# Moving operands in SBUF: new homes modulo 256 bytes for the context's tiles, the long operands and the first FFN's products

## The chip, the cores and the metric

The kernel runs on one core of a Trainium2 chip. A core has a matrix engine (TensorE, PE in the profile, with its weight loads listed apart as PEld), a vector engine (VectorE, DVE), a scalar engine (ScalarE, ACT), GpSimd (POOL), and queues for transfers between the chip's memory (HBM) and the on-chip buffer (SBUF). SBUF has 128 partitions; a tile is a range of bytes that is the same in each of them, and in this document its *home* is the byte address at which that range begins, often taken modulo 256. Sums of products go to PSUM. The metric is the device time of one execution in microseconds; of several executions the median counts.

## The reference

Two streams of tokens with 1024 features, 512 latent and 256 context tokens, go through two layers. Layer 0 mixes tokens by grouped-query attention (16 query heads, 4 key heads), layer 1 by a bidirectional Mamba-2 scan; a gated convolutional FFN of width 2816 follows each. All of it is float32.

```python
for i in range(2):
    h_l = rms_norm(x, w_mix[i]) * (1 + scale_l) + shift_l
    h_c = rms_norm(ctx, w_mix[i]) * (1 + scale_c) + shift_c
    o_l, o_c = attention(h_l, h_c) if i == 0 else mamba2(h_l, h_c)
    x += gate_l * o_l
    if i == 0: ctx += gate_c * o_c
    x += gate_l2 * ffn(modulated rms_norm of x)
    if i == 0: ctx += gate_c2 * ffn(modulated rms_norm of ctx)

def ffn(h):
    g, u = split(h @ w_up)              # 1024 -> 2 x 2816
    g = conv3(g) + b                    # along the tokens, per feature
    return (silu(g) * u) @ w_down       # 2816 -> 1024
```

The shifts, scales and gates come from two condition vectors (one for latent, one for context tokens) by a linear map per layer, six chunks of 1024 for each. The output is the latent stream `x`. The context is needed in the first layer and in the projections into the Mamba mixer, and no further.

## The kernel before

**Layout and products.** Activations lie feature-major: 8 tiles of 128 features by 512 latent or 256 context tokens. A float32 product is made of three products of rounded parts: weight and activation are each split into a rounded part and its remainder (`split`, L81 to L88: a cast on ACT, a subtraction on DVE), and `mm3` (L103 to L111) issues, for each block of 128 features, weight-high by activation-high (L108), weight-high by activation-low (L109), weight-low by activation-high (L111). The weight tile of 128 x 128 is loaded into TensorE for each of these; the activations (512 or 256 columns) move past it. In the profile `hh..` and `hl..` are the high and low parts of modulated activations, with the stage as the last letters: `a` attention, `f` FFN, `s` Mamba, `ol` and `oc` attention's output for latent and context tokens, `y` the first eight tiles of Mamba's output. `hdh`, `hdl` are the parts of the FFN's gated products, `yh`, `yl` those of the last eight tiles of Mamba's output.

**Rings.** Tiles come from pools. A tile that is asked for with a tag comes from a ring of a fixed number of buffers; a pool lays its rings and single tiles one behind the other in the order in which they are first asked for, each rounded up to 32 bytes, and a pool begins where the one before it ends. The pools in question, with the homes that the compiled program of the kernel before gives:

| pool and tile | bytes each x number | home modulo 256 |
|---|---|---|
| `const`: identity and selectors, parameters, ones, `sc32`, then 12 tiles `mod` and 4 `moda`, ... | `mod`: 64 x 12 | ends at 7264 |
| `p`, tag `h512`: long modulated tiles (latent tokens) | 2048 x 16 | 96 |
| `p`, tag `h256`: context's modulated tiles | 1024 x 16 | 96 |
| `p`, tag `t4`: weights as loaded, high, low | 4096 x 10 | 96 |
| `p`: `silu`, behind `t4` | 64 | 96 |
| `pa` (attention), `pf` (first FFN), `pg` (second FFN): all rings and tiles | multiples of 256 | 160 |
| `pt` (Mamba): `na`, one element, first in the pool | 32 | 160 |
| `pt`, tag `t3`: nine tiles of 3104 bytes | | eight residues 32 apart |
| `pt`, tag `t2`: 39 tiles of 2048 bytes, `yh` and `yl` among them | | 32 |

The pool `p` has a few small rings behind `silu`, and lasts for the whole kernel; `pa`, `pf`, `pt` and `pg` take turns in the space behind it.

**Order of work.** A scheduler orders each engine's instructions from the program as it is written (L406 to L515 of the attention are kept in the written order on PE, ACT and DVE). The stages, by time on the page's span: attention up to about 390 us; its output projection and the first FFN up to 972; the Mamba stage up to about 1500; the second FFN to the end.

- Attention (`attention`, L392): query and key projections `ps_l` for the latent and `ps_c` for the context tokens take their weights from slabs that lie in `pa`; four later query projections `ps_q` take them from `t4`. Attention's output projection is a `ps_d` with `hhol`, `hhoc`.
- FFN (`ffn`, L886): step `f` of 22 projects up twice (`ps_up`: 8 blocks x 3 terms of 512 columns, and in the first FFN the same of 256 columns for the context), convolves and gates on ACT and DVE into `hd` (L936 to L938), and splits `hd` into `hdh`, `hdl` (L939, L940). Latent and context tokens of the first FFN stand side by side in one tile of 768 columns, latent first. Two or three steps are a group, whose products are projected down (`down`, L856; `ps_d`) after the first up-projection of the next group. The last group is projected down in the order context, first latent half, second latent half (256 columns each), with the next norm interleaved; the first weights of the next stage read their halves as `ps_first`.
- Mamba (`ssd`, L969): `ps_in` is the projection in (six weight tiles for each of eight groups of heads, of which three, x twice and B, are for both streams), interleaved with the scan; `ps_wo` is the projection out, and sums eight tiles `y` in `h512` and eight in `pt`'s `t2` ring into one accumulation.

The condition chunks of layer 1 are computed by DVE during the first FFN (`ada_dve`, L156).

Of the kernel before, what the change touches and what calls it, by code (L numbers as in the profile page):

```python
# [7 lines left out]
P = 128  # L8
F32 = mybir.dt.float32
F32R = mybir.dt.float32r  # L10
# [6 lines left out]
KT = D // P  # L17
L = 512
C = 256
# [372 lines left out]
def attention(g, fill, X, late):  # L392
# [3 lines left out]
    S64 = slice(0, 64), slice(64, 128)  # L396
    Bk, Sb = (lambda name: Bank(g, name)), (lambda name: S(g, name))
    t2 = lambda name, dt=F32: g.t3p.tile([P, 512], dt, tag="t2", bufs=6, name=name)
    g.h = [[htiles(g, n, f"a{i}_{m}") for m in range(KT)] for i, n in enumerate((L, C))]
    hl, hc = g.h  # L400
    kn = g.par[:, PC["kn"] : PC["kn"] + 1]


# [52 lines left out]
    g.qn8 = g.const.tile([P, 1], F32, name="qn8")  # L456
    nc.vector.tensor_scalar(g.qn8, g.par[:, PC["qn"] : PC["qn"] + 1], HD ** -0.5, None, ALU.mult)

    e = g.p.tile([P, 2 * KT], F32, name="silu")
    nc.scalar.activation(e, g.cin, AF.Exp, scale=-1.0)  # L460
    nc.vector.tensor_scalar(e, e, 1.0, None, ALU.add)
    nc.vector.reciprocal(e, e)
# [423 lines left out]
def ffn(g, layer, streams, x, h, first, nxt=None, side=iter(()), after=()):  # L886

    nc, I = g.nc, g.I  # L890
    ns = len(streams)
    tot = sum(n for n, _ in streams)
    off = [0, L]

    cw = [g.par[:, PC[f"fw{layer}{t}"] : PC[f"fw{layer}{t}"] + NFT] for t in range(3)]
    cb = g.par[:, PC[f"fb{layer}"] : PC[f"fb{layer}"] + NFT]
    whole = [[(i, 0, n) for i, (n, _) in enumerate(streams)]]

    def gemm(t):

        if t % NFT == 0:
            ps = first[t // NFT]
        else:
            w = load_w(g, I["wup"][layer, t])
            if t % NFT == 1:
                out = []
                for i in range(ns):
                    ps = Bank(g, "ps_up1")
                    for _ in gemm_in(g, [(ps, w)], h, (0, 0), [[s] for s in whole[0] if s[0] == i]):
                        pass  # L910
                    out.append((ps, [i]))
                return [(ps[:, : streams[i][0]], off[i], off[i] + streams[i][0], i) for ps, (i,) in out]
            ps = S(g, "ps_up")
            for _ in gemm_in(g, [(ps, w)], h, off, [[s] for s in whole[0]]):
                pass
        return [(ps[:, :tot], 0, tot, None)]

    def up(f):
        pg = gemm(f)
        cv = t3(g, "cv", n=tot)  # L920
        w0, w1, w2 = (c[:, f : f + 1] for c in cw)
        for ps, a, b, _ in pg:
            nc.scalar.activation(cv[:, a:b], ps, AF.Identity, scale=w1, bias=cb[:, f : f + 1])
        for i in range(ns):
            a, b = off[i], off[i] + streams[i][0]
            ps, o = next((ps, o) for ps, o, e, j in pg if j in (None, i))
            nc.vector.scalar_tensor_tensor(cv[:, a + 1 : b], ps[:, a - o : b - o - 1], w0, cv[:, a + 1 : b], ALU.mult, ALU.add)
            nc.vector.scalar_tensor_tensor(cv[:, a : b - 1], ps[:, a - o + 1 : b - o], w2, cv[:, a : b - 1], ALU.mult, ALU.add)
        follow(g, nc.scalar.activation(cv, cv, AF.Silu))
        some = (2, 2, 2, 3)[f] if ns > 1 and f < 4 else 1  # L930
        for _ in range(some):
            next(side, None)
        pu = gemm(NFT + f)
        for _ in range(some):
            next(side, None)
        hd = t3(g, "hd", n=tot)  # L936
        for ps, a, b, _ in pu:
            nc.vector.tensor_tensor(hd[:, a:b], cv[:, a:b], ps, ALU.mult)  # L938
        hi, lo = t3(g, "hdh", F32R, n=tot), t3(g, "hdl", F32R, n=tot)  # L939
        split(g, hd, hi, lo)  # L940
        return [(hi[:, off[i] : off[i] + streams[i][0]], lo[:, off[i] : off[i] + streams[i][0]]) for i in range(ns)]

    gate = g.mod[layer][5]
    segs, f = [], 0
    for n in [3] + [2] * 8 + [3] if nxt else [2] * 11:
        segs.append(range(f, f + n))
        f += n
    acts, pend, wf = {}, None, []

    def flush(fs, order, norm=None, after=None):  # L950
        ws = [load_w(g, I["wdown"][layer, f * P : (f + 1) * P]) for f in fs]
        if after:
            wf.extend(firsts(g, *after))
        return down(g, ws, [acts.pop(f) for f in fs], gate, streams, x, order, norm, side=side)

    for fs in segs:
        for j, f in enumerate(fs):
            acts[f] = up(f)
            if j == 0 and pend:
                flush(pend, whole)  # L960
        pend = fs
    for _ in side:
        pass
    if nxt:
        ln_exp(g)
    return flush(pend, [[s] for s in ending(streams)], nxt, after), wf


def ssd(g, x, norm, wf, bg, close):  # L969
# [26 lines left out]

    H2 = 64
    ps = ps_dt
    na = small("na", [P, 1])
    follow(g, nc.scalar.activation(na, par("alog", 0), AF.Exp))  # L1000
    nc.vector.tensor_scalar(na, na, -1.0, None, ALU.mult)
    TH = T // 2
# [342 lines left out]
def body(nc, tc, I, out, dbg=None):  # L1345
# [25 lines left out]
    nc.vector.memset(g.sc32, 0.0)  # L1371
    tc.keep_in_program_order(nc.scalar.preload_act_table_set("natural_log_exp_and_others"))
    g.cin = g.par[:, PC["cc"] : PC["cc"] + 2 * KT]
    g.mod = [[g.const.tile([P, KT, 2], F32, name=f"mod{i}{c}") for c in range(6)] for i in range(2)]
    g.moda = [{c: g.const.tile([P, KT, 2], F32, name=f"moda{i}{c}") for c in (1, 4)} for i in range(2)]

    fill = Fill()
# [23 lines left out]
    first = first_tiles(g, wf, nrm, bg)  # L1401
    pha.close()
    phf = ExitStack()
    g.t3p, g.n3 = pool("pf", phf), 24


    def dump():
# [122 lines left out]
```

## Time and profile before

| | |
|---|---|
| median of 3 runs | 1873.63 us (1873.2 to 1874.46) |
| the profiled execution's own time | 1875.38 us |
| its span, first to last instruction | 1873.6 us |
| matmuls, busy time of TensorE | 11474, 1848.9 us (99%) |
| busy: weight loads, DVE, ACT, POOL | 1547.2, 1303.6, 807.3, 299.8 us |
| HBM read, written | 198.79 MB, 6.82 MB: 110 GB/s over the span |
| granted TensorE clock over the span | 0.998 |

The page names an instruction by line, engine, operation and `out<-in`, then its shape and count; behind the bar stand the group's busy time and the mean of one in ns, and then the idle time of the engine just before the group, with what ended it. A matmul's duration has the way through the array in it and overlaps the next one's; the distance from one start to the next is the pace.

### The profile page before, as it was taken

To read this page: it belongs to the slowest core of one execution; us is meant where nothing else is said; L and a number is where in the kernel's file an instruction comes from. 1 tells how busy PE (TensorE), PEld (TensorE's weight loads), DVE (VectorE), ACT (ScalarE), POOL (GpSimd) and SP (SyncE) were. 2 spreads that over 40 slices of the span, in tenths; PEclk is the share of its full clock that TensorE was granted. 3 is DMA by queue.
4 is the path that set the end of the run, shared out by engine and by line. 5 is a ranking of instruction groups with operands and counts; after the bars stand their busy time and mean duration, and the time that the engine had idled before them with its cause. 6 is when DMAs were issued, how large, how long until landed. Compare 5 with 4: busy or idle time off the path is not lost.

```text
span 1873.6 us, 28798 instructions
## 1 busy us (share of the span) xinstructions
PE 1848.9 (99%) x11474; PEld 1547.2 (83%) x11474; DVE 1303.6 (70%) x1950; ACT 807.3 (43%) x1402; POOL 299.8 (16%) x266
## 2 busy tenths in 40 slices
PE   9999999999999999999999999999999999999999
PEld 8876656798888888888888888888887888888887
DVE  6588888778787776544487787777797565565655
ACT  4534444363122222222367667776666352323231
POOL 2123120040000000000032333444443210000000
PEclk9999999999999999999999999999999999999999
DMA  9233151124444552211224432443352223222232
GB/s 345 76 109 101 63 178 52 57 84 164 146 135 145 191 185 99 68 58 56 68 91 141 124 105 87 124 124 113 124 178 93 79 91 97 95 95 97 90 103 89
DMA packets 74070, 211.67 MB, mean 113 GB/s; under 512 B 9040, under 2 KB 14544, under 8 KB 73808
## 3 DMA queue, kind: packets, MB, share of 16 engines
q1 hardware_dynamic: 73936, 209.84, 34.0%
q8 instruction: 90, 1.47, 0.3%
q14 instruction: 44, 0.36, 0.1%
HBM read 198.79 MB, written 6.82 MB: 110 GB/s over the span
## 4 chain that ended last, share of the span: by engine, by line
PE 84%; DVE 7%; issue 3%; DMA 2%; POOL 2%; ACT 2%; SPq 0%; DVEq 0%; POOLq 0%; ACTq 0%
PE ps_up L108 10%; PE ps_up L111 10%; PE ps_up L109 10%; PE ps_d L108 6%; PE ps_d L111 6%; PE ps_d L109 6%; PE ps_in L111 4%; PE ps_in L109 4%; PE ps_in L108 4%; PE ps_s L697 2%; PE ps_o L661 2%; PE ps_st L1123 2%; DMA wada<-in_adaA 1%; PE ps_wo L111 1%; PE ps_wo L108 1%
## 5 line engine op out<-in xcount | busy, mean ns | idle before, releaser
L87 DVE TENSOR_TENSOR wl<-wst,wh 128x1024 fp32r<-128x1024 f32 x207 | 258.5, 1249 | 233.9 <-PE ps_up L109 138.9
L85 ACT CAST wh<-wst 128x1024 fp32r<-128x1024 f32 x211 | 221.3, 1049 | 393.7 <-DMA wst<-in_wup 323.6
L108 PE MATMUL ps_up<-hhf,wh 128*128 128x512 f32 x1008 | 357.6, 355 | 0.0
L109 PE MATMUL ps_up<-hlf,wh 128*128 128x512 f32 x1008 | 357.3, 354 | 0.0
L111 PE MATMUL ps_up<-hhf,wl 128*128 128x512 f32 x1008 | 357.0, 354 | 0.0
L108 PEld LDWEIGHTS ps_up<-hhf,wh 128*128 128x128 f32 x1008 | 190.8, 189 | 26.4
L109 PEld LDWEIGHTS ps_up<-hlf,wh 128*128 128x128 f32 x1008 | 190.8, 189 | 26.3
L111 PEld LDWEIGHTS ps_up<-hhf,wl 128*128 128x128 f32 x1008 | 190.6, 189 | 26.4
L108 PE MATMUL ps_in<-hhs,wh 128*128 128x512 f32 (+1 forms) x560 | 204.4, 365 | 1.5 <-ACT dt L1008 1.5
L109 PE MATMUL ps_in<-hls,wh 128*128 128x512 f32 (+1 forms) x560 | 199.4, 356 | 0.0
L111 PE MATMUL ps_in<-hhs,wl 128*128 128x512 f32 (+1 forms) x560 | 198.7, 355 | 0.0
L108 PE MATMUL ps_d<-hdh,wh 128*128 128x512 f32 (+1 forms) x568 | 193.3, 342 | 0.2 <-ACT hdh L85 0.2
L111 PE MATMUL ps_d<-hdh,wl 128*128 128x512 f32 (+1 forms) x568 | 193.5, 341 | 0.0
L109 PE MATMUL ps_d<-hdl,wh 128*128 128x512 f32 (+1 forms) x568 | 192.9, 340 | 0.3 <-DVE hdl L87 0.3
L874 DVE SCALAR_TENSOR_TENSOR X<-ps_d,mod,X 128x512 f32<-128x512 f32 (+1 forms) x224 | 124.3, 583 | 35.9 <-PE ps_d L111 35.2
L108 PEld LDWEIGHTS ps_in<-hhs,wh 128*128 128x128 f32 x560 | 105.9, 189 | 16.6 <-ACT dt L1008 1.7
L109 PEld LDWEIGHTS ps_d<-hdl,wh 128*128 128x128 f32 x568 | 106.7, 188 | 14.8 <-DVE hdl L87 0.7
L111 PEld LDWEIGHTS ps_in<-hhs,wl 128*128 128x128 f32 x560 | 105.8, 189 | 14.7
L111 PEld LDWEIGHTS ps_d<-hdh,wl 128*128 128x128 f32 x568 | 106.6, 188 | 13.1
L108 PEld LDWEIGHTS ps_d<-hdh,wh 128*128 128x128 f32 x568 | 106.3, 188 | 13.4 <-ACT hdh L85 0.7
L109 PEld LDWEIGHTS ps_in<-hls,wh 128*128 128x128 f32 x560 | 106.0, 189 | 13.2
L700 ACT ACTIVATE pr<-ps_s 128x1024 f32<-128x1024 f32 x56 | 57.2, 1021 | 107.2 <-PE ps_s L699 107.2
(339 smaller groups left out, 3653.4 us busy)
## 6 DMA issues: line engine op xcount, KB each, us to landing
wst<-in_wup SPq DMA_DIRECT2D x88, 512.0 KB, 3.3
wada<-in_adaT SPq DMA_DIRECT2D x56, 512.0 KB, 3.3
wst<-in_win SPq DMA_DIRECT2D x48, 512.0 KB, 3.4
wst<-in_wdown SPq DMA_DIRECT2D x44, 512.0 KB, 3.5
E<-ad SPq DMA_DIRECT2D x64, 256.0 KB, 6.9
wada<-in_adaB SPq DMA_DIRECT2D x24, 512.0 KB, 4.1
ec<-ead SPq DMA_DIRECT2D x64, 128.0 KB, 5.6
wst<-in_wout SPq DMA_DIRECT2D x16, 512.0 KB, 3.3
```

The lines of the kernel that those rows point to most:

```text
L85: cast = keep(nc.scalar.copy(hi, src))
L87: keep(eng.tensor_tensor(lo, src, _r(hi), ALU.subtract))
L108: mm(out, wh, ah, start=first, stop=False)
L109: mm(out, wh, al, start=False, stop=False)
L111: mm(out, wl, ah, start=False, stop=last)
L661: nc.tensor.matmul(po[S64[e], :n], v, pr[:, 512 * e + off : 512 * e + off + n], start=first, stop=last)
L697: nc.tensor.matmul(outs[e], kk[e][a][S64[e], k], b[S64[e], q], start=i == 0, stop=False)
L700: exps.append(nc.scalar.activation(pr, ps, AF.Exp))
L874: nc.vector.scalar_tensor_tensor(ap, o[:, c0:c1], gate[:, m, v : v + 1], ap, ALU.mult, ALU.add)
L1123: nc.tensor.matmul(ps[:, d * 256 : (d + 1) * 256], Bt[:, t * P : (t + 1) * P], xw[d][t], start=t == ts[0], stop=t == ts[-1])
```

## The change

Nothing of the arithmetic changes. Five edits alter where tiles lie:

- the three modulation tiles `mod` 3, 4, 5 of layer 1 (64 bytes each) are asked for in pool `p`, between the long and the context tiles, instead of in `const`;
- `silu` (64 bytes) is asked for ahead of everything in `t4`, instead of behind it;
- `hdh` and `hdl` come from a ring of their own of 11 tiles; the `t3` ring of the first FFN goes from 24 tiles to 14 (the second FFN's stays at 24);
- in the first FFN a gap of 48 elements (192 bytes) stands between the latent and the context part of `hdh` and `hdl`, and the two parts are split by a cast and a subtraction each, instead of one of each for both;
- `na`, the Mamba pool's first tile, is asked for with 40 elements, of which one is used.

```diff
@@ attention
-    g.h = [[htiles(g, n, f"a{i}_{m}") for m in range(KT)] for i, n in enumerate((L, C))]
-    hl, hc = g.h
+    hl = [htiles(g, L, f"a0_{m}") for m in range(KT)]
+    for ch in (3, 4, 5):
+        g.mod[1][ch] = g.p.tile([P, KT, 2], F32, name=f"mod1{ch}")
+    hc = [htiles(g, C, f"a1_{m}") for m in range(KT)]
+    e = g.p.tile([P, 2 * KT], F32, name="silu")
+    g.h = [hl, hc]
...
-    e = g.p.tile([P, 2 * KT], F32, name="silu")
     nc.scalar.activation(e, g.cin, AF.Exp, scale=-1.0)
@@ ffn, up(f)
-        hi, lo = t3(g, "hdh", F32R, n=tot), t3(g, "hdl", F32R, n=tot)
-        split(g, hd, hi, lo)
-        return [(hi[:, off[i] : off[i] + streams[i][0]], lo[:, off[i] : off[i] + streams[i][0]]) for i in range(ns)]
+        gap = 48 * (ns - 1)
+        pair = [g.t3p.tile([P, (tot + gap + 63) // 64 * 64], F32R, tag="hd", bufs=11, name=nm) for nm in ("hdh", "hdl")]
+        hls = []
+        for i in range(ns):
+            a, b = off[i], off[i] + streams[i][0]
+            hls.append(tuple(t[:, a + i * gap : b + i * gap] for t in pair))
+        if ns == 1:
+            split(g, hd, *hls[0])
+            return hls
+        for i in range(ns):
+            split(g, hd[:, off[i] : off[i] + streams[i][0]], *hls[i])
+        return hls
@@ ssd
-    na = small("na", [P, 1])
+    na = small("na", [P, 40])[:, :1]
@@ body
-    g.mod = [[g.const.tile([P, KT, 2], F32, name=f"mod{i}{c}") for c in range(6)] for i in range(2)]
+    g.mod = [[g.const.tile([P, KT, 2], F32, name=f"mod{i}{c}") for c in range(3 if i else 6)] + [None] * (3 * i)
+             for i in range(2)]
...
-    g.t3p, g.n3 = pool("pf", phf), 24
+    g.t3p, g.n3 = pool("pf", phf), 14
```

## The prediction

> **What bounds the kernel now.** I read the page's busy times first, then the chain that ended last, then the busy time by stage, then the waits of TensorE. On the page, the busy shares and the chain's shares by engine; below them, by stage (window, its length, busy us and instruction count of PE, PEld, DVE, ACT, POOL, then clock and DMA), the first FFN and the Mamba stage; last, two of the longest waits of PE in the whole run (its total, how often, the longest once).
>
> ```profile
> PE 1848.9 (99%) x11474; PEld 1547.2 (83%) x11474; DVE 1303.6 (70%) x1950; ACT 807.3 (43%) x1402; POOL 299.8 (16%) x266
> PE 84%; DVE 7%; issue 3%; DMA 2%; POOL 2%; ACT 2%; SPq 0%; DVEq 0%; POOLq 0%; ACTq 0%
> 410.00:925.00 515.00, 514.69 (x2987) 454.80 (x2986) 339.16 (x516) 128.80 (x139) 1.48 (x2) 1.00 0.36 123
> 972.00:1400.00 428.00, 423.90 (x2499) 367.10 (x2498) 327.12 (x379) 296.61 (x627) 155.96 (x135) 1.00 0.40 121
> PE ps_xt L1097 <- DVE xf L1200: 1.8, 6, 0.5
> PE ps_ada L132 <- DMA wada<-in_adaA: 1.8, 1, 1.8
> ```
>
> TensorE is busy 99% of the span, its clock is granted in full (1.00 in both stages), and no wait in that list sums to more than 1.8 us. In the first FFN it lacks 0.3 us of 515, in the Mamba stage 4.1 us of 428. So the kernel ends when TensorE has issued its matmuls, and the only thing that moves the end is the pace of back-to-back matmuls: time per matmul times their number. This decides how I cost the change: nothing in it alters the number of matmuls, so I look for what sets their pace.
>
> **The pace depends on where the operands lie.** The compiled program of the kernel before gives every tile's address. All three-term products (L108, L109, L111) read their weights from the ring `t4`, which lies at 96 modulo 256 bytes. The moving operands lie at 96 too (tags h512 and h256: difference 0 from the weights), at 160 (tiles of the attention and FFN pools: difference 64) or at 32 (the Mamba pool's 2 KB ring: difference 192). Below, groups of the same shape (columns: instruction, its operands, its shape, count; busy us, mean ns of one). I take the L109 row of each trio; the L108 and L111 rows have the same counts.
>
> ```profile
> L109 PE MATMUL ps_up<-hlf,wh 128*128 128x512 f32 x672 | 262.2, 390 | 0.0
> L109 PE MATMUL ps_up<-hlf,wh 128*128 128x256 f32 x336 | 95.1, 283 | 0.0
> L109 PE MATMUL ps_in<-hls,wh 128*128 128x256 f32 x184 | 52.0, 283 | 0.0
> L109 PE MATMUL ps_first<-hlf,wh 128*128 128x256 f32 x80 | 22.8, 290 | 2.3 <-POOL hlf L301 1.5 <-DVE hlf L304 0.8
> L109 PE MATMUL ps_d<-hloc,wh 128*128 128x256 f32 x64 | 18.0, 283 | 0.0
> L109 PE MATMUL ps_q<-hla,wh 128*128 128x256 f32 x32 | 9.0, 281 | 0.0
> L109 PE MATMUL ps_c<-hla,wsh 128*128 128x256 f32 x48 | 13.3, 277 | 0.0
> L109 PE MATMUL ps_d<-hdl,wh 128*128 128x256 f32 x256 | 71.0, 279 | 0.3 <-DVE hdl L87 0.3
> L111 PE MATMUL ps_d<-hdh,wl 128*128 128x512 f32 x312 | 122.6, 393 | 0.0
> L109 PE MATMUL ps_l<-hla,wsh 128*128 128x512 f32 x48 | 19.8, 413 | 0.3 <-DVE hla L304 0.3
> L109 PE MATMUL ps_wo<-hly,wh 128*128 128x512 f32 x48 | 18.7, 390 | 0.0
> L109 PE MATMUL ps_wo<-yl,wh 128*128 128x512 f32 x48 | 18.9, 394 | 0.0
> L109 PE MATMUL ps_wo<-hly,wh 128*128 128x256 f32 x32 | 9.0, 282 | 0.0
> L109 PE MATMUL ps_wo<-yl,wh 128*128 128x256 f32 x32 | 8.9, 277 | 0.0
> ```
>
> Two pairs are controls. `ps_c` and `ps_q` read the same context tiles in the same stage; against the slabs (difference 192) one takes 277 ns, against `t4` (difference 0) 281. In `ps_wo` the tiles `hy` (difference 0) and `y` (192) are read by one accumulation with weights from one ring. There the order turns round with the width: of 256 columns the tile at 192 is quicker (277 against 282), of 512 columns the tile at 0 is (390 against 394). A row's mean has the pipeline's latency in it, so for the pace itself I take starts in the instructions by time. In `ps_wo` each run below is 24 matmuls long (8 blocks by 3 terms); the two `ps_up` rows bound one run of 24 in the first FFN.
>
> ```profile
> 903.45 0.28 PE L108 MATMUL ps_up<-hhf,wh 128*128 128x256 f32 x1
> ...
> 906.33 0.40 PE L108 MATMUL ps_up<-hhf,wh 128*128 128x512 f32 x1
> ...
> 1472.55 0.39 PE L108 MATMUL ps_wo<-yh,wh 128*128 128x512 f32 x1
> ...
> 1478.15 0.28 PE L108 MATMUL ps_wo<-hhy,wh 128*128 128x256 f32 x1
> ...
> 1481.02 0.29 PE L108 MATMUL ps_wo<-yh,wh 128*128 128x256 f32 x1
> ...
> 1483.76 0.28 PE L108 MATMUL ps_wo<-hhy,wh 128*128 128x256 f32 x1
> ...
> 1486.62 0.29 PE L108 MATMUL ps_wo<-yh,wh 128*128 128x256 f32 x1
> ```
>
> 256 columns at difference 0: 2.88 us / 24 = 120.0 ns in `ps_up`, 2.87 and 2.86 us / 24 = 119.4 in `ps_wo`. 256 columns at 192: 2.74 / 24 = 114.2 ns. 512 columns at 192: 5.60 / 24 = 233.3 ns. So a 256-column matmul gains 120.0 - 114.2 = 5.8 ns by going from 0 to 192, and a 512-column one about 4 ns a row by going the other way.
>
> A rule of the Trainium skill speaks against all this: in "TensorE: Matmul & The Clock Gate", section "Step-by-step: what each phase is for", TensorE has two independent SBUF read ports, and "Loading the next tile's weights doesn't steal SBUF read bandwidth from the running matmul". By that the homes would not matter and the sum below would be zero. The rows of `ps_wo` differ by 5 ns within one accumulation, so here I go by the rows; the rule is a rival further down.
>
> **The change part by part: where each operand lands.** A pool lays its tiles in order of first request. (1) Three modulation tiles of 64 bytes leave the constants and are asked for between the long and the context tiles, so the pool that holds h512, h256 and `t4` starts 192 bytes lower. h512 goes from 96 to 160. (2) h256 comes behind the three tiles and stays at 96. (3) The 64-byte `silu` tile now comes ahead of `t4`, which goes from 96 to 160. The sum of sizes is the same, so the pools behind do not move. Differences after: h512 to `t4` 160 - 160 = 0 as before, h256 to `t4` 96 - 160 = -64, which is 192 (before 0). Tiles of the attention and FFN pools stay at 160: difference 0 (before 64), and h512 against the slabs also 0 (before 192). (4) `na` grows from one to 40 elements (32 to 160 bytes), so the Mamba pool's ring goes from 32 to 160: `y` is at 0 (before 192). (5) The products `hdh`, `hdl` get a ring of their own; in the first FFN the context part is written 48 elements (192 bytes) later, so it lies at 192 (before 64).
>
> None of this adds an instruction or a DMA but (5), which splits each of the first FFN's products in two.
>
> **The sum**, counts times three for the three terms:
>
> - Context by h256, 0 to 192: `ps_up` 336 x 3 = 1008; `ps_in` 184 x 3 = 552; `hoc` 64 x 3 = 192; `ps_q` 32 x 3 = 96; of `ps_first` the context part, 2 weight tiles x 8 blocks in each of two stages, 2 x 16 x 3 = 96. Together 1944 x 5.8 ns = 11.3 us. The other 256-column `ps_first` (64 of the row's 80) are halves of the latent tokens, which stay at 0.
> - Long `hd`, 64 to 0: 312 x 3 = 936, 393 against 390 ns at most and equal rows at least: I take 2 ns, 1.9 us (0 to 2.8).
> - `hd` of 256 columns: 22 x 8 x 3 = 528 are context, 64 to 192. They stand at 279 with target 277, but come in runs of six to nine, too short for a settled pace: I take 0 (0 to -1.1 us). The other 240 are latent halves of the two last groups, 64 to 0: 279 to 283 is +4 ns, 1.0 us lost.
> - `y`: 48 x 3 = 144 long gain 4 ns (0.6 us), 32 x 3 = 96 short lose 5 ns (0.5 us): 0.1 gained.
> - `ps_l`: 144 long, 192 to 0. At 413 ns a row this stage is not at its pace (the wait for the modulation loads above lies in it): 4 ns each would be 0.6, I take 0.3 (0 to 0.6).
> - What else changes its residue (the Mamba stage's transposes against the constants) I take at 0: the ring they read has nine tiles at eight residues 32 bytes apart, and a shift by 128 leaves the same eight.
>
> Sum: 11.3 + 1.9 - 1.0 + 0.1 + 0.3 = 12.6 us, and 0.4 of the span between 0 and 1.1 for the context `hd`: 13 us.
>
> **The split products.** On DVE and ACT (columns as above, idle time and its releaser last):
>
> ```profile
> L87 DVE TENSOR_TENSOR hdl<-hd,hdh 128x768 fp32r<-128x768 f32 x22 | 20.9, 951 | 5.4 <-ACT hdh L85 5.4
> L87 DVE TENSOR_TENSOR hdl<-hd,hdh 128x512 fp32r<-128x512 f32 x22 | 15.0, 682 | 1.4 <-ACT hdh L85 1.4
> L85 ACT CAST hdh<-hd 128x768 fp32r<-128x768 f32 x22 | 18.4, 837 | 86.4 <-DVE hd L938 86.4
> L85 ACT CAST hdh<-hd 128x512 fp32r<-128x512 f32 x22 | 13.7, 621 | 46.7 <-DVE hd L938 46.7
> L938 DVE TENSOR_TENSOR hd<-cv,ps_up 128x256 f32<-128x256 f32 x1 | 0.4, 414 | 0.0
> PE ps_d L109 <- DVE hdl L87: 0.3, 1, 0.3
> PE ps_d L108 <- ACT hdh L85: 0.2, 1, 0.2
> ```
>
> A DVE subtraction of 768 becomes 682 ns and, by the row with 256 columns, at most 414: +145 ns a step, 22 steps, 3.2 us. ACT is alike (621 and at most 414 against 837: +198 ns, 4.4 us). DVE idles 515 - 339 = 176 us in this stage and ACT 386, and the products of a group are read a whole up-projection later, so PE does not see it. That cover is gone once, in the last group, where PE now waits 0.2 and 0.3 us for these two: bounds -0.3 to +0.4 us, taken at 0, since the subtraction of the latent part may start before the context's cast is done.
>
> Of the rings: `t3` falls from 24 to 14 tiles, but a step takes only two of them (`cv`, `hd`), and the products have 11 of their own, five pairs, where the pending group holds two or three and the next one has one or two in the making. I take 0.
>
> So the profiled execution, 1875.38 us (span 1873.6 and 1.8 around it), would go to 1875.4 - 13.0 = 1862.4. It stands 1.75 above the median of the runs, 1873.63, and the median goes to 1860.6.
>
> **Rivals.**
>
> *The gain of the Mamba stage doesn't arrive.* There ACT and DVE are busy 297 and 327 of 428 us and PE waits 4.1 us; PE's faster `ps_in` could turn into longer waits for `xf` and the E tiles. 552 x 5.8 = 3.2 us less: 1863.8. Against it: the waits are spread thin (0.5 us the longest for `xf`). Chance 0.08.
>
> *The smaller rings bite.* At the first FFN's end squares, accumulators and `ht` tiles share 14 buffers where 24 were. If each of the 8 x 3 column blocks waited 0.3 us, 7 us go: 1867.8. Against it: a block leaves one square and one `ht` behind. Chance 0.05.
>
> *Homes do not matter, the pace belongs to the stage.* The weights' loads and the moving tiles would not disturb each other, the 5.8 ns would not appear, and only the split remains, within 0.4 us: 1873.6. For it: `ps_c` and `ps_q` differ in more than the home of their weights. Against it: they read one tile, and `hy` and `y` stand in one accumulation. The same result would follow if the layout did not come out as worked above. Chance 0.04. The port rule of the Trainium skill, cited above from "TensorE: Matmul & The Clock Gate", would give this result.
>
> *Slower: 192 is a bad place for context operands too.* In the rows of 512 columns the tile at 192 is the slower by 4 ns a matmul. If that price were one per weight load and the quick 256-column rows had another cause, 1944 context matmuls would pay 4 to 6 ns more, 7.8 to 11.7 us, less the 1.7 won elsewhere in the sum: 1873.6 + 8 = 1881.6. It decides once the context pace passes 120.0 + 1.7 us / 1944 = 120.9 ns. Against it: 277 and 114.2 ns in both short groups at 192. Chance 0.04.
>
> **How the numbers follow.** The forecast has 0.79, the rivals 0.08, 0.05, 0.04 and 0.04. The lower end: all context matmuls at 113 ns (7.0 x 1944 = 13.6) with every other term at its best (2.8 - 1.0 + 1.1 + 0.1 + 0.6 + 0.3 = 3.9) is 17.5: 1856.1. The upper end takes in the first rival and most of a second loss, a gain of 6.6: 1867. About 0.2% (3.7 us) is what a measurement can tell from no change. Faster by more: the forecast, the first rival and most of the second, 0.89; within: 0.06; slower: 0.05.
>
> **What would show it.** Right: `ps_up` and `ps_in` of 256 columns fall from 283 to 277 ns, `hoc` and `ps_q` too, while `ps_up` of 512 stays at 390; `yl` of 512 goes to 390 and of 256 to 282; `ps_d` of 512 to 390 or 391; a run of 24 context matmuls in the first FFN spans 2.74 us instead of 2.88; PE's busy share stays at 99%. Wrong: `ps_up` of 256 columns still at 283 (homes don't matter), or at 285 and over (192 is bad), or PE waits for `hd`, `cv` or `ht` that the list of waits does not have now.

## The result, and the profile after

The changed kernel takes 1868.21 us (median of 6 runs, 1865.96 to 1869.35) against 1874.05 us of the kernel before beside it: a ratio of 0.9965, 95% interval [0.9953, 0.9978]. Timed twice more against the kernel before it had 0.9957 [0.9942, 0.9971] and 0.9961 [0.9948, 0.9975]. The differences of the medians are 5.8, 8.5 and 6.9 us. So it is faster, by about half of the 13 us that the prediction's sum gave (0.45 to 0.65 of it); 1868.2 lies above its upper end, 1867.0.

Of the changed kernel: the page's busy times; the two stage windows that the prediction quoted; and the one wait of TensorE for the split products that the list of waits still has.

```profile
PE 1841.1 (99%) x11474; PEld 1542.8 (83%) x11474; DVE 1305.0 (70%) x1972; ACT 809.6 (43%) x1424; POOL 304.3 (16%) x266
```

```profile
410.00:925.00 515.00, 514.73 (x3013) 457.10 (x3013) 343.10 (x541) 132.41 (x163) 1.43 (x2) 1.00 0.37 124
972.00:1400.00 428.00, 425.21 (x2501) 367.12 (x2500) 331.79 (x381) 298.70 (x631) 163.99 (x139) 1.00 0.40 123
```

```profile
PE ps_d L108 <- ACT hdh L85: 0.2, 1, 0.2
```

The number of matmuls is the same, TensorE is busy for 99% as before, and in both windows it has no more idle time than before (0.27 of 515 us, 2.8 of 428 us). In the same 515 us it starts 3013 matmuls instead of 2987: the gain is a shorter distance between starts, and nothing waits anew. The groups of the changed kernel that answer to those of the prediction (columns as there):

```profile
L109 PE MATMUL ps_up<-hlf,wh 128*128 128x512 f32 x672 | 261.4, 389 | 0.0
L109 PE MATMUL ps_d<-hdl,wh 128*128 128x512 f32 x312 | 121.4, 389 | 0.0
L109 PE MATMUL ps_up<-hlf,wh 128*128 128x256 f32 x336 | 94.4, 281 | 0.0
L109 PE MATMUL ps_d<-hdl,wh 128*128 128x256 f32 x256 | 71.9, 282 | 0.0
L109 PE MATMUL ps_in<-hls,wh 128*128 128x256 f32 x184 | 51.4, 279 | 0.0
L109 PE MATMUL ps_l<-hla,wsh 128*128 128x512 f32 x48 | 19.8, 412 | 0.4 <-DVE hla L304 0.3
L109 PE MATMUL ps_wo<-yl,wh 128*128 128x512 f32 x48 | 18.7, 389 | 0.0
L109 PE MATMUL ps_d<-hloc,wh 128*128 128x256 f32 x64 | 17.6, 277 | 0.0
...
L109 PE MATMUL ps_c<-hla,wsh 128*128 128x256 f32 x48 | 13.4, 279 | 0.0
L109 PE MATMUL ps_wo<-yl,wh 128*128 128x256 f32 x32 | 9.0, 283 | 0.0
L109 PE MATMUL ps_q<-hla,wh 128*128 128x256 f32 x32 | 8.9, 279 | 0.0
```

`hoc` (`hloc`) has the 277 ns that was forecast for all context rows. The two large ones stop short: `ps_up` of 256 columns at 281 and `ps_in` at 279. `ps_c` lies at 192 from its weights before and after, and has gone from 277 to 279; what changed is the run ahead of it, whose 512 columns went from 192 to 0. That is the first sign that the home alone does not fix the pace.

The paces are better read from starts. In the instructions of the changed kernel by time, a long run of 24 and the context run of 24 behind it:

```profile
455.18 0.39 PE L108 MATMUL ps_up<-hhf,wh 128*128 128x512 f32 x1
...
460.62 0.28 PE L108 MATMUL ps_up<-hhf,wh 128*128 128x256 f32 x1
...
463.45 0.39 PE L108 MATMUL ps_d<-hdh,wh 128*128 128x512 f32 x1
```

2.83 us / 24 = 117.9 ns for the context (forecast 114.2, before 120.0), 5.44 / 24 = 226.7 for the long ones. In the trace's own ns all 42 context runs of `ps_up` lie at 117.8 ns from the first matmul to the last.

Where the time went, as differences of sums of start-to-start distances between the two profiled executions (us, worked out from all starts of a group):

| group | change | forecast |
|---|---|---|
| context by h256: `ps_up` -1.92, `ps_in` -1.93, `hoc` -0.72, `ps_q` -0.21, `ps_first` -0.57 | -5.35 | -11.3 |
| long `hd` | -2.63 | -1.9 |
| `hd` of 256 columns | +1.88 | +0.6 |
| `ps_up` of 512 columns | -2.38 | 0 |
| `ps_in` of 512 columns | +0.49 | 0 |
| `y` | -0.47 | -0.1 |
| `ps_l` | 0.0 | -0.3 |
| everything else (start and attention) | -0.93 | 0 |
| sum | -9.39 | -13.0 |

Three rows hold more than they say. Of `ps_up` of 512 columns, 1.18 us lie in the first FFN. The other 1.20 lie in the second FFN, which has no context runs: 0.50 behind long `hd` runs, and 0.70 in its first 96 matmuls, where the execution of before had a lower clock (below). Of `ps_first`, 0.34 us of the 0.57 fall at that same place, so they are not the context's either. Of `hd` of 256 columns, +1.36 us are the context's and +0.52 the latent halves'.

The spans differ by 9.4 us and the medians by 5.8, since the profiled execution of before lay about 1.3 us above its median here and that of after 2.3 below its own. What moves between executions of one kernel are groups of the start, the attention stage and the first matmuls of the second FFN, by 0.5 to 1 us each. Much of this is the granted clock, the column behind the counts in the windows. Here are the same 100 us before and after:

```profile
1500.00:1600.00 100.00, 97.25 (x475) 82.02 (x474) 62.29 (x101) 38.98 (x57) 4.12 (x5) 0.98 0.29 95
```

```profile
1500.00:1600.00 100.00, 97.88 (x461) 81.58 (x461) 60.98 (x96) 38.04 (x52) 1.65 (x2) 1.00 0.28 91
```

The 0.98 is one stretch: from 1512 to 1515 us the clock of before is 0.50. The traces of the other runs show such stretches too, mostly 3.4 us long: ahead of the last 2 us of the span none to three in an execution, at 15 to 20, near 60, 115 or 278, or at 1505 to 1518 us. The five further executions of the changed kernel go with the clock of the whole: 1864.21 us at 1.000, 1870.13 at 0.997. The context runs of `ps_up` have no part in this: they sum to 118.72 us in all three profiled executions of the changed kernel.

### The profile page after: what moved, and what is told of

Its sections match the earlier page's. It is cut to its first block, busy times and chain, and to the rows that moved or that the text cites. A ratio compares the mean times of both kernels' runs of the same rounds, so it can differ in the third digit from the quotient of the medians.

```text
span 1864.2 us, 28839 instructions
## 1 busy us (share of the span) xinstructions
PE 1841.1 (99%) x11474; PEld 1542.8 (83%) x11474; DVE 1305.0 (70%) x1972; ACT 809.6 (43%) x1424; POOL 304.3 (16%) x266
## 4 chain that ended last, share of the span: by engine, by line
PE 84%; DVE 7%; issue 3%; ACT 2%; POOL 2%; DMA 2%; SPq 0%; DVEq 0%; POOLq 0%; ACTq 0%
PE ps_up L111 10%; PE ps_up L109 10%; PE ps_up L108 10%; PE ps_d L108 7%; PE ps_d L109 6%; PE ps_d L111 6%; PE ps_in L111 4%; PE ps_in L109 4%; PE ps_in L108 4%; PE ps_s L700 2%; PE ps_o L664 2%; PE ps_st L1135 2%; PE ps_wo L111 1%; PE ps_wo L108 1%; PE ps_wo L109 1%
```

## The experiments

The theory at the outset: the pace belongs to the difference of homes, but a 256-column matmul at 192 has two steady paces, 113.3 and 117.8 ns, and what ran just before it decides which (the *entry*). Two sights from the kernel before led to it, both of 256 columns at 192: `ps_c` behind 512 columns at 192, and `y` behind 256 columns at 0. The rows show them, and between them a long run at 0 behind a context run at 0.

```profile
64.71 0.28 PE L108 MATMUL ps_c<-hha,wsh 128*128 128x256 f32 x1
...
67.44 0.28 PE L108 MATMUL ps_c<-hha,wsh 128*128 128x256 f32 x1
...
457.21 0.40 PE L108 MATMUL ps_up<-hhf,wh 128*128 128x512 f32 x1
...
458.37 0.39 PE L111 MATMUL ps_up<-hhf,wl 128*128 128x512 f32 x1
...
462.68 0.28 PE L108 MATMUL ps_up<-hhf,wh 128*128 128x256 f32 x1
...
1481.38 0.28 PE L108 MATMUL ps_wo<-yh,wh 128*128 128x256 f32 x1
...
1481.72 0.28 PE L108 MATMUL ps_wo<-yh,wh 128*128 128x256 f32 x1
```

`ps_c`: 2.73 / 24 = 113.8 ns, from its second matmul on. The `y` run starts at 1481.02 (the prediction's row) with 0.36 us for its first three, 120 ns each, and from 1481.72 to 1483.76 takes 2.04 / 18 = 113.3. The prediction's 114.2 was the mean of this run: a number with an entry of its own in it. The long run: the first five take 1.16 us, 232 ns each, and all 24 5.47, 227.9; in the changed kernel 226.7. So a context run can also leave a debt to the run behind it.

**Homes 64 and 128 for the context.** Of the three `mod` tiles, one or two instead of three stand ahead of the context tiles, and the gap shrinks alike.

```diff
-    for ch in (3, 4, 5): ...                 # ahead of hc
+    mods((3,))        # second kernel: mods((3, 4))
     hc = [htiles(g, C, f"a1_{m}") for m in range(KT)]
+    mods((4, 5))      # second kernel: mods((5,))
...
-        gap = 48 * (ns - 1)
+        gap = 16 * (ns - 1)      # second kernel: 32
```

> The changed kernel with the context's tiles (h256 and the context part of the first FFN's products) at 64 instead of 192 from the weights; long operands stay at 0. Theory (entry): a run of 256-column matmuls holds one pace from its first matmul to its last, and which of a few paces it is (113.3, 117.8 or 120 ns) depends on the home and on what ran just before it; behind 512 columns at 0 I expect one value in all 42 runs of the first FFN, which the kernel before can't tell. At 113.3 the row of ps_up with 256 columns is near 277 and the kernel takes 1868 - 1536 x 4.5 ns = 1861 us; at 117.8 it is near 281 and 1868; at 120 near 283 and 1872. Rival (the home alone sets the pace): as the products at 64 in the kernel before, a mixture with mean 115.8 ns, row 279, 1865 us.

> The changed kernel with the context's tiles at 128 from the weights; long operands stay at 0. No run so far shows 128. Theory (entry): again one pace in all 42 runs of ps_up, from the same three values: row 277 and 1861 us, 281 and 1868, or 283 and 1872. Rival (the home alone, the farther from the weights the better): 128 is the farthest, so 113.3 ns, row 277, 1861 us.

64 bytes: 1874.15 us, ratio 0.9998 [0.9989, 1.0007]. 128 bytes: 1877.26 us, 1.0013 [1.0005, 1.0022]. One row of each, context of `ps_up`, and one of the long `hd` or `ps_up` behind it:

```profile
L108 PE MATMUL ps_up<-hhf,wh 128*128 128x512 f32 x672 | 262.3, 391 | 0.0
...
L109 PE MATMUL ps_up<-hlf,wh 128*128 128x256 f32 x336 | 93.8, 279 | 0.0
```

```profile
L109 PE MATMUL ps_d<-hdl,wh 128*128 128x512 f32 x312 | 122.3, 392 | 0.0
L109 PE MATMUL ps_up<-hlf,wh 128*128 128x256 f32 x336 | 95.4, 284 | 0.0
```

At 64 the context of `ps_up` is as quick as at 192 (sums of distances 118.86 and 118.72 us, though the row's mean is 279 against 281: a mean duration is not the pace). But the long groups are slower: `ps_up` +1.65, `hd` +1.72 against the changed kernel. At 128 everything is: context of `ps_up` +2.06, `ps_in` +1.48, long `ps_up` +2.41, long `hd` +2.60. With the smaller groups that read moved tiles or stand behind them these are some 6 and 11 us, the right size for the medians 1874 and 1877 against 1867 to 1868. Both medians lie above every time that was set down, 1872 at most: neither reading priced the runs behind. So 192 is better than 64 less for its own pace than for what it leaves to the long runs.

**Entries.** In the first FFN's up-projections of two streams the context run is entered in six ways in turn. Nothing is left out; the d-kinds add one matmul whose result is overwritten, the s-kinds cut the second context matmul in two.

```diff
+    if kind[0] == "d":
+        nc.tensor.matmul(o[:, :n], w[0][:, :P], h[1][0][0][:, :n], start=True, stop=True)
...
+    if k == 0 and cut:
+        mm(o[:, :cut], wh, al[:, :cut], start=False, stop=False)
+        mm(o[:, cut:], wh, al[:, cut:], start=False, stop=False)
```

> The changed kernel; in the first FFN the 24 context matmuls of a weight tile are entered in six ways in turn: as they are, behind an extra matmul of 32, 64 or 128 columns whose sums are overwritten, or with the second matmul cut into 64 + 192 or 128 + 128 columns. Homes, neighbours and stage are the same. Theory (entry): the pace of the rest of a run is 113.3 or 117.8 ns, constant within the run and the same for all runs of one kind; at least one kind goes over to 113.3 while the uncut ones stay at 117.8. Rival (the stage, its traffic on the other engines, sets 117.8): all kinds stay at 117.8. Rival (the home alone): likewise.

Instructions of this kernel by time: a run with its second matmul cut at 64, and a plain one.

```profile
495.83 0.28 PE L935 MATMUL ps_up<-hhf,wh 128*128 128x256 f32 x1
...
496.30 0.28 PE L935 MATMUL ps_up<-hhf,wh 128*128 128x256 f32 x1
...
498.69 0.39 PE L108 MATMUL ps_up<-hhf,wh 128*128 128x512 f32 x1
...
512.46 0.28 PE L935 MATMUL ps_up<-hhf,wh 128*128 128x256 f32 x1
...
515.28 0.39 PE L108 MATMUL ps_up<-hhf,wh 128*128 128x512 f32 x1
```

Behind the cut the last 21 matmuls take 2.39 us, 113.8 each; the plain run takes 2.82, 117.5. Over all repeats, which agree to 1 ns: plain 2827 ns and 117.8 throughout; one extra of 64 columns 2858 to 2859, and both cuts 2858 to 2859, settled at 113.3; an extra of 32 or of 128 columns 2937 to 2938 and still at 117.8. Same tiles, same homes, same stage: two paces, chosen by the entry. With this fell the two other readings, that 117.8 belongs to the stage or that the home alone sets it. But an extra or a cut costs more than it wins: 31 ns a run at the least.

**Long operands at 192.** The `mod` tiles go behind the weights' ring, so that the long operands lie at 192 from the weights and the context stays there (the long part of `hd` comes to 192 too, its context part to 128).

```diff
-    for ch in (3, 4, 5):                     # ahead of hc
-        g.mod[1][ch] = g.p.tile([P, KT, 2], F32, name=f"mod1{ch}")
...
+    for ch in (3, 4, 5):                     # behind t4's first request
+        g.mod[1][ch] = g.p.tile([P, KT, 2], F32, name=f"mod1{ch}")
```

> The changed kernel with the long modulated tiles at 192 from the weights too (the context's stay at 192; the FFN's products, whose pool stays where it is, come to 192 for the long part and 128 for the context). Theory (entry): as in ps_c of the kernel before, a context run behind 512 columns at 192 goes at 113.3 ns: ps_up of 256 columns 277, while its 512 columns go to 233.3 ns, row 396; some 4440 long matmuls x 6.5 ns = +29 us, 2256 short ones at -4.3 ns = -10: near 1887 us. Rival (stage or home alone): the context runs keep 117.8 ns and the row 281, near 1891 us.

1888.41 us, one run. Two plain context runs of it by time:

```profile
454.49 0.28 PE L108 MATMUL ps_up<-hhf,wh 128*128 128x256 f32 x1
...
457.32 0.39 PE L108 MATMUL ps_up<-hhf,wh 128*128 128x512 f32 x1
...
496.57 0.28 PE L108 MATMUL ps_up<-hhf,wh 128*128 128x256 f32 x1
...
499.30 0.39 PE L108 MATMUL ps_up<-hhf,wh 128*128 128x512 f32 x1
```

2.83 us and 2.73 us for the same 24 matmuls, 117.9 and 113.8 ns, in one kernel and one stage. This is half a miss: the entry reading set down 113.3 ns for every context run behind 512 columns at 192 and a row at 277, and only 8 of the 42 runs have it; 34 go at 117.8, and the row stands at 280. Both kinds stand behind long matmuls of one shape and home, so naming the group ahead is too coarse. The starts show a finer sign: the long run at 192 alternates between distances of 231 and 236 ns, and all 8 quick runs stand behind a last long matmul of 236, all 34 others behind one of 230 or 231. That is a sight in one trace, not a test. The long price of the prediction holds in the large: `ps_up` of 512 columns goes from 226.8 to 233.4 ns (+13.15 us over 2016), `hd` +6.0 and `ps_in` +5.15. The long tiles stay at 160 modulo 256 here, only the weights have moved (160 to 224); and `ps_up` of 512 columns settles at 226.7 ns with both at 96 and with both at 160. So it is not the moving tile's own home alone that counts.

**The changed kernel again, and without the gap.** The second has no gap and one split, so that the context part of `hd` lies at 0.

```diff
-        gap = 48 * (ns - 1)
-        pair = [...]; two splits
+        hi, lo = (g.t3p.tile([P, tot], F32R, tag="hd", bufs=11, name=nm) for nm in ("hdh", "hdl"))
+        split(g, hd, hi, lo)
```

> The changed kernel itself, more executions and another profiled one, to see what differs between executions and how much of the 9.4 us between the first two profiled spans is the change. If the paces are locked by what ran before (entry), the matmul rows of the FFN and Mamba stages repeat to 1 ns and the executions differ in the attention stage alone: median 1867 to 1869. If the paces are drawn anew in each execution, ps_up of 256 columns lies anywhere between 277 and 281 and ps_d of 512 between 389 and 393.

> The changed kernel without the gap and with one split for both parts of the first FFN's products (their own ring of 11 stays): the context's 528 products go from 192 to 0. Theory (entry): they leave 117.8 for 120 ns at most, 2.2 x 528 = 1.2 us slower, less what the undivided split saves in the last group (0.3): 1869, which can't be told from the changed kernel's 1868.2. Rival (the gap carries the gain as planned, 192 worth 5.8 ns): 3 us slower, 1871.

1867.34 us, 0.9957 [0.9942, 0.9971], and 1869.48 us, 0.9968 [0.9956, 0.9981]. The rows without the gap are 1.48 us more for long `hd`, 0.78 for `hd` of 256 columns; the intervals of the whole overlap. The 256-column products, which the gap moved, lose 0.78 us: the entry reading set down 1.2 at most, the rival 3. The gap is worth about 2 us in the trace, and nearly two thirds of it in the long runs behind, not in the runs that it moves.

**Scan of homes.** The first FFN's context up-projections read scratch tiles at eight differences in turn. These kernels leave out the context's own up-projection; number, shape and order of the matmuls stay.

```diff
+                o = 8 * (tiles[0] % 8)        # second kernel: 1, 2, 4, 6, 10, 12, 14, 52 elements
+                at = tuple(t[:, o : o + C] for t in scan)
+                for _ in gemm_in(g, [(ps, w)], [None, [at] * KT], off, segs[1:]):
```

> Leaves out the first FFN's context product: in its 40 up-projection tiles the context matmuls read two scratch tiles in place of the modulated context, at 0, 32, 64 ... 224 from the weights in turn, so that the context's result is not the reference's; number, shape and order of the instructions stay. Each run of 24 is entered behind 512 columns at 0. Theory (entry and home together): each home has one pace in all its five runs; 0, 64, 128 and 192 repeat 120, 117.8, 120 and 117.8, and of the four homes not yet seen at most one or two lock at 113.3. Rival (distance alone): the pace falls steadily from 0 to 128 and rises again.

> Leaves out the first FFN's context product, as the scan of homes did, but with the scratch tiles read at 4, 8, 16, 24, 40, 48, 56 and 208 bytes from the weights in turn. Theory (entry and home): each home has one pace, the same in its five runs, between 2720 (24 x 113.3) and 2882 ns a run; 32 had 2803. If the pace is set by lines of 32 bytes or more, 4 to 24 go like 0 (2873) and 40 to 56 like 32 (2803); if by single words, they differ among themselves.

Differences 32 and 192, by time in the first kernel:

```profile
445.11 0.28 PE L108 MATMUL ps_up<-sch,wh 128*128 128x256 f32 x1
...
447.92 0.39 PE L108 MATMUL ps_up<-hhf,wh 128*128 128x512 f32 x1
...
511.57 0.28 PE L108 MATMUL ps_up<-sch,wh 128*128 128x256 f32 x1
...
514.39 0.39 PE L108 MATMUL ps_up<-hhf,wh 128*128 128x512 f32 x1
```

The two rows' distances, 2.81 and 2.82 us, are rounded to 10 ns; in the trace's own ns they are 2803 and 2826. In ns, a run of 24 behind 512 columns at 0, the same to 1 ns in every repeat:

| bytes | 0 | 4 | 8 | 16 | 24 | 32 | 40 | 48 | 56 |
|---|---|---|---|---|---|---|---|---|---|
| ns | 2873 | 2940 | 2880 | 2850 | 2879 | 2803 | 2878 | 2846 | 2882 |

| bytes | 64 | 96 | 128 | 160 | 192 | 208 | 224 |
|---|---|---|---|---|---|---|---|
| ns | 2830 | 2882 | 2875 | 2854 | 2827 | 2861 | 2839 |

The differences follow no simple line, so the rival by which distance alone counts falls, and 4 bytes matter (2873 against 2940). No home goes at 113.3 ns behind 512 columns at 0. For the run alone 32 bytes is the quickest, by 24 ns. The same traces hold the debt that it leaves: taken with the 24 long matmuls behind it, a run is 8267 ns at 32 and 8267 at 192, 8300 at 16 and at 160, 8306 at 64, 8340 at 0, 8360 at 128 and 8433 at 4. So for the pair 32 wins nothing over 192.

**The quickest home of the scan.** Context at 32 in the whole kernel, by smaller tiles ahead of it and a gap of 8 elements.

```diff
-    for ch in (3, 4, 5): ...
+    g.mod[1][3] = mod(3, 1)                  # 32 bytes
     hc = [htiles(g, C, f"a1_{m}") for m in range(KT)]
+    g.mod[1][4], g.mod[1][5] = mod(4, 2), mod(5, 2)
+    g.p.tile([P, 8], F32, name="pad")
...
+        gap = 8 * (ns - 1)
```

> The changed kernel with the context's tiles (h256 and the context part of the first FFN's products) at 32 from the weights in place of 192; long operands stay at 0. Theory (entry and home): ps_up's runs of 24 go from 2826 to 2803 ns as in the scan, 42 x 23 ns = 1.0 us, the products' 528 at 116.7 in place of 117.8 another 0.6, and ps_in, which enters its runs in several ways and was at 116.1, stays within 0.5 us: 1866, 1 to 2 us below the changed kernel's 1867.3 to 1868.2. Rival (a home at 32 unsettles the long runs behind it, as 64 did, where ps_d of 512 columns went from 389 to 392): 1872.

1870.11 us, 0.9972 [0.9961, 0.9983], between what the two readings gave (1866 and 1872). Its rows:

```profile
L109 PE MATMUL ps_up<-hlf,wh 128*128 128x512 f32 x672 | 262.2, 390 | 0.0
...
L109 PE MATMUL ps_d<-hdl,wh 128*128 128x512 f32 x312 | 122.1, 391 | 0.0
L109 PE MATMUL ps_up<-hlf,wh 128*128 128x256 f32 x336 | 93.8, 279 | 0.0
```

Context of `ps_up` -1.01 us as the scan says; long `ps_up` +1.04, long `hd` +1.69 behind it. The first two cancel, as the pairs of the scan said; a scan that is read by the run alone doesn't see the debt.

**Orders.** If the entry decides, the order of the same matmuls should do it without an added or cut one. Six orders of the 24 long and 24 context matmuls in turn.

```diff
+    order = {"none": lo + co,
+             "one1": lo[:-1] + co[:1] + lo[-1:] + co[1:],
+             "one2": lo[:-2] + co[:1] + lo[-2:] + co[1:],
+             "two1": lo[:-1] + co[:2] + lo[-1:] + co[2:],
+             "blk1": lo[:-3] + co[:3] + lo[-3:] + co[3:],
+             "alt3": lo[:-3] + [m for p in zip(co[:3], lo[-3:]) for m in p] + co[3:]}[kind]
```

> The first FFN's up-projections of two streams (40 pairs of 24 long and 24 context matmuls) are issued in six orders in turn; the matmuls, their operands and their homes are those of the changed kernel, nothing is added. none: 24 long, 24 context. one1: the first context matmul stands ahead of the last long one. one2: ahead of the last two. two1: the first two context matmuls ahead of the last long one. blk1: the first block of context (3) ahead of the last block of long (3). alt3: these six in turn. Entry theory (which of two paces 256 columns at 192 keep, 113.3 or 117.8 ns, is set by what ran just before): every repeat of one order takes the same time to some ns, and the orders fall into groups: those that leave the remaining context matmuls at 113.3 ns end the pair up to 21 x 4.5 = 95 ns earlier than none, less what the changes between widths cost (a change cost about 31 ns net in the scan of entries). Then at least one order gives a pair of 48 below the 24 x 226.7 + 24 x 117.8 = 8268 ns of none. Rival (the entry is set by a matmul of another width being cut or added, not by the order): the context matmuls stay at 117.8 ns in all orders, and each mixed order is 0 to 60 ns longer than none. Whole kernel: by the rival 1868 to 1870 us, by entry 1866 to 1869 us; the times of the pairs decide, not the whole.

All repeats of one2, one context matmul ahead of the last two long ones, go on at 113.4 ns; all of the other five orders at 117.8. The pairs that no other matmul interrupts take 8191 to 8214 ns by one2, 8266 to 8312 by the plain order, 8277 to 8278 by one1, 8285 to 8286 by two1, 8267 to 8290 by blk1, 8288 to 8289 by alt3. Each has the debt of the pair ahead in it: two1 always stands behind one2, and its first three long matmuls take 231 to 232 ns.

**That order in every pair**, then once more beside the changed kernel on one chip.

```diff
+    lo, co = runs
+    for o, a, b, first, last in lo[:-2] + co[:1] + lo[-2:] + co[1:]:
+        mm(o, a, b, start=first, stop=last)
```

> The changed kernel, with the first context matmul of every two-stream up-projection of the first FFN (40 pairs of 24 long and 24 context matmuls) issued ahead of the last two long ones, and nothing else. In the scan of orders this one order left the remaining context matmuls at 113.4 ns instead of 117.8, and a pair of 48 took 8191 to 8214 ns where the plain order took 8266 to 8312. Entry theory: all 40 pairs settle at 113.3 to 113.4 ns and gain 52 to 98 ns each, 2.1 to 3.9 us in all; the ps_up rows of 256 columns go down from 281 to 277 or 278 ns, and the median from 1867.8 to about 1864.8 us (ratio to the kernel before 0.993 to 0.995). Rival (what the context runs win the long runs behind them pay back, as with the homes at 32 and 64 bytes): the pair still gains in the scan's sense, but the rows of ps_up and ps_d of 512 columns go up by 1 ns and more, and the median stays within 1 us of 1867.8. Slower than the changed kernel would be the result if the long runs behind a context run at 113.3 ns lost over 100 ns each.

> The kernel with the first context matmul ahead of the last two long ones, again, timed beside the changed kernel on the same chip. Entry theory: the trace gave 3.7 us less for the 256-column rows of ps_up and 1.2 us more for the 512-column rows behind them, 2.5 us net, so the median lies 1.5 to 3.5 us below that of the changed kernel beside it. Rival (the first time was the scatter of the start and of the attention stage): the two medians agree within 1 us, though the rows of ps_up differ.

> The changed kernel itself, unaltered, beside the kernel with one context matmul ahead. 1867 to 1869 us by its earlier medians (1868.21 and 1867.34). Entry theory: 1.5 to 3.5 us above the other. Rival: within 1 us of it.

Instructions by time in the first of these. The row "x2" is a long matmul and the context one behind it, which have the same names:

```profile
455.95 0.39 PE L389 MATMUL ps_up<-hhf,wh 128*128 128x512 f32 x1
...
456.64 0.39 PE L389 MATMUL ps_up<-hhf,wh 128*128 128x512 f32 x1
...
460.72 0.51 PE L389 MATMUL ps_up<-hhf,wh 128*128 128x512 f32 x2
461.06 0.40 PE L389 MATMUL ps_up<-hlf,wh 128*128 128x512 f32 x1
461.30 0.40 PE L389 MATMUL ps_up<-hhf,wl 128*128 128x512 f32 x1
461.54 0.28 PE L389 MATMUL ps_up<-hlf,wh 128*128 128x256 f32 x1
...
464.15 0.39 PE L108 MATMUL ps_d<-hdh,wh 128*128 128x512 f32 x1
```

The remaining 23 context matmuls take 2.61 us, 113.5 ns each, in all pairs of the trace. Paid for it: the two long ones behind the first context matmul (0.24 each), and the first three of the long run behind a context run at 113.4 (455.95 to 456.64: 0.69, 230 ns each, 232 in the trace's own ns). Against the changed kernel the `ps_up` groups have -3.73 and +1.17 us, 2.6 net, and long `hd` pays 0.2 of it. An uninterrupted pair takes 8191 to 8208 ns, debt included, where it took 8267.

In time this is 1864.34 us, 0.9947 [0.9934, 0.9960], the lowest median of the study; but beside the changed kernel 1865.88 (1865.55 to 1866.80) against 1866.75 (1866.18 to 1867.37): 0.9 us. By what was set down this is the rival's case (within 1 us), though the rows show the mechanism again (`ps_up` of 256 columns -3.73; long `ps_up` +1.19 in the first FFN; `hd` +0.22). In that pair of executions the start of the kernel, not the FFN, took most of it back: `ps_ada` has +1.28 us, `ps_l` +0.79 and the warm-up -0.85. For the largest of these the traces show the clock again: all of the 1.28 falls between 114 and 118 us, where the granted clock is 0.57 in the one execution and 1.00 in the other. Over the whole, the five executions of each kernel have clocks of 0.997 to 0.999, so the clock does not tell why the medians lie only 0.9 us apart. That the order wins 2.3 us in its stage, the runs behind included, is shown; that the kernel is faster than the changed one by as much is not.

## Why the prediction was right in kind and wrong in size

**What bounds the kernel: right.** The end follows the distance between starts, in both stages; TensorE stays at 99%.

**Where the operands lie: right in kind.** The paces moved with the homes, at the same matmuls in the same order. The rival that homes do not matter falls with the rows of 512 columns (`yl` 394 to 389, `hdh` 393 and `hdl` 391 to 389) and, within one stage, with the scan of homes: 2803 to 2940 ns for the same 24 matmuls.

By the rule of the Trainium skill named there ("TensorE: Matmul & The Clock Gate", section "Step-by-step: what each phase is for", two independent read ports) these would be equal; this case's trace doesn't agree, by up to 137 ns in a run of 24.

**The step that failed** is "So a 256-column matmul gains 120.0 - 114.2 = 5.8 ns by going from 0 to 192", and with it the term "1944 x 5.8 ns = 11.3 us", which came out at 5.35 at most. The 114.2 was measured on runs behind 256 columns at 0, and was set beside `ps_c` (277 ns), which stands behind 512 columns at 192. The 1008 matmuls that bore half of the sum stand behind 512 columns at 0. There the pace came to 117.8, from 120.0 in the prediction's row and 119.7 over the whole run, so the term for `ps_up` was 1.9 instead of 5.85 us. `ps_in` enters from scan matmuls, some of its runs settle at 113.3 and others at 117.8, and it won 1.9 of 3.2; `hoc` with 277 ns won 0.7 of 1.1. The trace of before held two warnings: the first matmuls of the `y` run at 120 ns, the rest at 113.3; and the runs of six and nine of the context's `hd`, which the prediction held too short for a settled pace. Of the 72 such runs ahead of the last group, 51 go at 113.3 ns and 21 at 117.8, all of one shape and home.

**"`ps_up` of 512 stays at 390": wrong, in the kernel's favour.** Its home did not change, but its forerunner's did: the first five behind a context run at 0 took 228 to 236 ns (28 ns above pace in a run of 24), behind 192 they take 226.7. That is 1.2 us in the first FFN that no step of the sum had. In the second FFN the same happens behind long `hd`, which went from 64 to 0: 0.5 us. The other 0.7 us of the table's row are the clock's and not the change's. That these gains fell the right way, and hid part of what the context lacked, was luck.

**Long `hd`, 64 to 0:** 2.6 us for 1.9, a term in the right place. **`hd` of 256 columns:** the latent halves lost 0.5 us where 1.0 was set down. The context part, taken at 0 to 1.1 gained, lost 1.4: at 64 behind 512 at 64 its short runs went at 114.7 ns on the mean, at 192 behind 512 at 0 at 117.8. A gain from the gap comes by way of the long runs, as the kernel without it shows. **`y`, `ps_l`:** signs as forecast or nothing; `yl` 390 and 282 forecast, 389 and 283 found.

**The costs taken at nothing: right.** DVE has 3.9 us more in the first FFN's window and ACT 3.6, and TensorE's wait for the last products is 0.2 us where it was 0.2 and 0.3. No wait for `cv`, `hd` or `ht` has come: the smaller rings do not bite, and that rival falls. The gain of the Mamba stage did arrive as far as the pace allowed: TensorE idles there less than before. The slower case, 192 as a bad place, would have needed 120.9 ns.

**The range** ended at 1867.0 because its bounds let every pace at 192 be 113 to 114.2. The pace at 192 behind long matmuls at 0 had not been seen in any trace; with a bound of 120 ns for it the range would have reached the result.

## What to carry to other kernels

A pace is a property of a sequence, not of an operand. Before a pace from one group is used to price another, compare what runs ahead of each, and see whether the first matmuls of a run go at the same pace as the last; and price the run behind as well. Where a kernel lives on back-to-back matmuls, homes of operands are worth a scan in place (here 2803 to 2940 ns for one run), judged together with the run behind and then by the whole kernel.

## What the runs showed of the hardware

- 256 columns at 192 bytes have two steady paces, 113.3 and 117.8 ns, that hold for the rest of a run of 24 and are chosen by what ran before: an extra of 64 columns, a cut of the second matmul, or one context matmul ahead of the last two long ones gives the first; extras of 32 and 128 columns, and five other orders, leave the second.
- 512 columns have 226.7 ns at 0 and 233.4 at 192 (231 and 236 in turn), and the first three to five behind a context run pay 1 to 9 ns each, or nothing, by that run's home and pace.
- The differences go down to single words: 2873 ns at 0 bytes, 2940 at 4, 2880 at 8.
- In stretches of 3.4 us, none to three of them in an execution ahead of its last 2 us, the granted clock is 0.50; the ones that were followed here, at 114 and at 1505 to 1515 us, moved a group by 0.5 to 1.3 us each.

What in the chip makes these paces was not found: the runs show on what they depend, not by which resource. Nor do the runs show why the clock is halved in one execution and not in the next.
